# Gate and up products by blocks (seven products for eight) from the third chunk on, two of four sums of weight blocks by accumulating DMAs

## The chip, the cores and the metric

One core of one Trainium2 chip runs the whole program. The metric is device microseconds of one execution, from start to end; lower is better. The engines are TensorE (PE), VectorE (DVE), ScalarE (ACT), GpSimd (POOL) and SyncE (SP); each works through its own row of instructions in order, and they wait for each other by semaphores.

## The reference

Two decoder layers on 512 tokens of width 1024 in float32: a gated short convolution in the first, dilated window attention in the second, and behind each a gated feed-forward part, which is what the change touches:

```python
def swiglu(x, w_gate_up, w_down):
    g, u = jnp.split(x @ w_gate_up, 2, axis=-1)
    return (jax.nn.silu(g) * u) @ w_down
...
    f = swiglu(rms_norm(h, ffn_norm_pre[layer]), ffn_w_gate_up[layer], ffn_w_down[layer])
    h = h + rms_norm(f, ffn_norm_post[layer])
```

Here x is 512 x 1024, w_gate_up is 1024 x 5632 (gate and up, 2816 columns each) and w_down is 2816 x 1024.

## The kernel before

Every product keeps float32 accuracy by splitting both operands in two fp32r parts, a high one (a cast on ACT) and a low one (a subtraction on DVE): `split` (L91), and `parts` (L104) for weights. A product is then three matmuls: high by high, low by high, high by low. The input x lies in SBUF by features, as `xh` and `xl` in tiles of 128 features by 128 tokens.

`ffn` (L394) walks through 11 chunks of 256 gate columns and the 256 up columns that belong to them. `load_cols` (L124) fetches each 1024 x 256 piece by one DMA of 1 MB on SP into `raw`, of which there are two buffers (`wp`). `makers` (L197) splits it in halves of 128 columns, and `feature_mm` (L135, matmuls in L160) makes the products: for each half 8 pieces of features x 3 matmuls, 128 columns of weights standing, 512 tokens moving, gate and up in turn, each into a PSUM bank of its own (tags mm and at, four banks each). For one half of a chunk ACT makes the silu and DVE the product with up:

```python
                    s = apool.tile([P, T], F32, tag="silu", name="s", bufs=2)
                    nc.scalar.activation(s, ps[2 * j], AF.Silu)
                    nc.vector.tensor_tensor(act[2 * c + j], ps[2 * j + 1], s, ALU.mult)
```

The first chunk is made in token halves, between which the last two transposes of x (`Next.x`, L326) are put (`Next.rest`, L337). After the chunks `down` (L348) multiplies by w_down. Split weights lie in tiles with six buffers each of high and low.

A scheduler sets each engine's row when the program is built; matmuls issued through `strict` (L130) stay in the order of the code. A semaphore holds back an instruction and with it all that stands behind it on its engine.

Of the kernel before, what the change touches and what calls it, by code (L numbers as in the profile page):

```python
# [15 lines left out]
P = 128  # L16
# [22 lines left out]
def trunk(  # L39
# [27 lines left out]

    xp = [keep.tile([P, KT * T], F32R, name=n, align_bytes=LINE) for n in ("xh", "xl")]  # L70
# [5 lines left out]
    cst = keep.tile([P, 576], F32, name="cst")  # L76
# [11 lines left out]
    def bank(tag, name):  # L88
        return psum.tile([P, T], F32, tag=tag, name=name)
# [14 lines left out]
    def parts(src, gain=None, pool=wp, bufs=6):  # L104


        _, a, b = src.shape
        wh = pool.tile([P, a, b], F32R, tag="wh", name="wh", bufs=bufs, align_bytes=LINE)
        wl = pool.tile([P, a, b], F32R, tag="wl", name="wl", bufs=bufs, align_bytes=LINE)
        if gain is None:  # L110
            split(wh, wl, src)
            return wh, wl
        for i in range(a):
            g = gain[:, i:i + 1]
            nc.scalar.mul(wh[:, i], src[:, i], g)  # L115
            nc.vector.scalar_tensor_tensor(  # L116
                wl[:, i], src[:, i], g, wh[:, i].bitcast(F32), ALU.mult, ALU.subtract)
        return wh, wl
# [272 lines left out]
                    after.after_half(tt, n)  # L391
        return after

    def ffn(layer, pending, after):  # L394
        w = ffn_w_gate_up[layer]
        with ExitStack() as phase:
            apool = phase.enter_context(tc.tile_pool(name=f"a{layer}", bufs=4))
            act = []
            for n, bufs in ((1, NF - 12), (0, 12)):
# [3 lines left out]
                act = [pool.tile([P, T], F32, tag=f"act{k}", name="act")  # L403
                       for k in range(bufs)] + act
            for c in range(NF // 2):
                rg = load_cols(w, c * 256)
                ru = load_cols(w, DFF + c * 256)
                mg, mu = makers("mm", rg), makers("at", ru)
                rest = pending.rest() if c == 0 else {}
                if c == 1:  # L410
                    rest["marks"] = [pending.made[NT - 1]] * 4
                ps = feature_mms([mg[0], mu[0], mg[1], mu[1]], **rest)
                for j in range(2):
                    s = apool.tile([P, T], F32, tag="silu", name="s", bufs=2)
                    nc.scalar.activation(s, ps[2 * j], AF.Silu)  # L415
                    nc.vector.tensor_tensor(act[2 * c + j], ps[2 * j + 1], s, ALU.mult)  # L416
# [14 lines left out]
    with ExitStack() as phase:  # L431
# [57 lines left out]
        for c in range(KT // 2):  # L489
# [58 lines left out]
    pending = ffn(0, pending, lambda ys: Next(npool, ys, ffn_norm_post[0], None))  # L548

# [380 lines left out]
```

## Time and profile before

| | |
|---|---|
| median of 3 runs | 1476.7 us (1476.43 to 1477.5) |
| profiled execution | 1476.04 us, its span 1474.3 us |
| PE busy | 1459.1 us, 99% of the span |
| DVE / ACT / POOL busy | 692.6 / 657.8 / 57.3 us |
| DMA traffic | 137.44 MB, mean 93 GB/s |

The rows in the section further down come from several views. The page gives sums over the execution. The stage table gives for each stretch (start:end, length) the busy time and number of instructions of PE, PE's weight loads, DVE, ACT and POOL, then the mean granted clock of PE (1.00 is full), the share of the DMA engines and GB/s. The timeline gives start, duration, engine, line, operation, output<-inputs, shape and number of instructions merged in one row; in brackets the idle time before and what ended it. The groups by line give count, then busy us and mean ns of one. Durations of neighbours overlap: what an engine can do in a row shows in the distance of the starts.

### The profile page before, as it was taken

Reading aid. Unit: us, or ns where it says so; the run is one execution under the profiler, and the core shown is the slowest. Engines: PE = TensorE matmul, PEld = TensorE weight load, DVE = VectorE, ACT = ScalarE, POOL = GpSimd, SP = SyncE. Lnnn points to the kernel's source line nnn. Section 1 sums busy time; section 2 is a strip of 40 time slices with the busy share of each in tenths; the row PEclk is TensorE's granted clock in tenths of the full one; section 3 lists DMA queues with packets and bytes.
Section 4 is the critical chain, followed back from the end, with each engine's and each line's share of the span. In section 5 each row is a group of like instructions: output and inputs, shape, how many; then the busy total and the mean of one; then the engine's idle time right before and its main releaser. Section 6 shows DMA issues by size and latency. Waiting matters only on the chain.

```text
span 1474.3 us, 20308 instructions
## 1 busy us (share of the span) xinstructions
PE 1459.1 (99%) x8160; PEld 1247.3 (85%) x8160; DVE 692.6 (47%) x1381; ACT 657.8 (45%) x1337; POOL 57.3 (4%) x108
## 2 busy tenths in 40 slices
PE   9999999999999999999999999999999999999998
PEld 7888898888888889898899889889789888888886
DVE  5644453232223446767457555745545323223433
ACT  4313342222222336896677768768444222222321
POOL 1000100000000010010000001001010000000000
PEclk9999999999999999999999999999999999999999
DMA  6333123233232312322212312312113331332311
GB/s 217 114 116 114 57 91 107 89 114 103 83 127 102 116 56 70 125 66 92 94 46 87 111 62 60 115 58 60 58 58 115 114 110 62 114 128 94 107 57 57
DMA packets 110516, 137.44 MB, mean 93 GB/s; under 512 B 3502, under 2 KB 99286, under 8 KB 110423
## 3 DMA queue, kind: packets, MB, share of 16 engines
q1 hardware_dynamic: 108852, 135.69, 28.0%
q8 instruction: 64, 1.05, 0.3%
q0 software_dynamic: 1280, 0.26, 0.3%
q14 instruction: 30, 0.24, 0.1%
q10 hardware_dynamic: 290, 0.20, 0.0%
HBM read 133.92 MB, written 2.23 MB: 92 GB/s over the span
## 4 chain that ended last, share of the span: by engine, by line
PE 72%; issue 25%; DVE 1%; POOL 1%; ACT 1%; DMA 0%; SPq 0%; POOLq 0%; DVEq 0%; ACTq 0%
PE mmf L133 16%; PE atf L160 15%; PE mmf L160 12%; PE vps L133 10%; PE s L133 2%; PE tr L133 2%; PE o L133 2%; PE y L133 1%; PE tr L283 1%; PE y2b L231 0%; PE y3b L231 0%; PE y2b L227 0%; PE y3b L227 0%; PE y3b L229 0%; PE y2a L231 0%
## 5 line engine op out<-in xcount | busy, mean ns | idle before, releaser
L94 DVE TENSOR_TENSOR wl<-raw,wh 128x1024 fp32r<-128x1024 f32 x176 | 210.7, 1223 | 70.1 <-ACT wh L93 69.7
L93 ACT CAST wh<-raw 128x1024 fp32r<-128x1024 f32 x176 | 178.1, 1046 | 75.9 <-PE atf L160 43.1
L160 PE MATMUL atf<-xh,wh 128*128 128x512 f32 (+1 forms) x560 | 181.0, 366 | 0.0
L160 PE MATMUL atf<-xh,wl 128*128 128x512 f32 (+1 forms) x560 | 180.4, 365 | 0.0
L160 PE MATMUL atf<-xl,wh 128*128 128x512 f32 (+1 forms) x560 | 180.0, 365 | 0.0
L415 ACT ACTIVATE s<-mmf 128x512 f32<-128x512 f32 x44 | 26.3, 598 | 330.3 <-PE mmf L160 322.1
L416 DVE TENSOR_TENSOR act<-atf,s 128x512 f32<-128x512 f32 x44 | 30.4, 692 | 297.3 <-ACT s L415 297.3
L116 DVE SCALAR_TENSOR_TENSOR wl<-raw,cols,wh 128x256 fp32r<-128x256 f32 x272 | 115.8, 483 | 104.2 <-ACT wh L115 104.2
L160 PE MATMUL mmf<-xh,wh 128*128 128x512 f32 (+1 forms) x496 | 162.1, 365 | 0.6 <-ACT xh L93 0.6
L160 PE MATMUL mmf<-xl,wh 128*128 128x512 f32 (+1 forms) x496 | 160.4, 362 | 0.0
L160 PE MATMUL mmf<-xh,wl 128*128 128x512 f32 (+1 forms) x496 | 160.3, 362 | 0.0
L115 ACT ACTIVATE wh<-raw,cols 128x256 fp32r<-128x256 f32 x272 | 115.0, 498 | 65.5 <-PE mmf L133 46.9
L160 PEld LDWEIGHTS atf<-xh,wh 128*128 128x128 f32 x560 | 99.6, 189 | 16.7
L160 PEld LDWEIGHTS atf<-xh,wl 128*128 128x128 f32 x560 | 99.6, 189 | 16.8
L160 PEld LDWEIGHTS atf<-xl,wh 128*128 128x128 f32 x560 | 99.5, 189 | 16.9
L133 PE MATMUL mmf<-xh,wh 128*128 128x512 f32 x352 | 110.7, 396 | 0.0
L133 PE MATMUL mmf<-xh,wl 128*128 128x512 f32 x352 | 108.8, 390 | 0.0
L133 PE MATMUL mmf<-xl,wh 128*128 128x512 f32 x352 | 108.5, 390 | 0.0
L160 PEld LDWEIGHTS mmf<-xh,wh 128*128 128x128 f32 x496 | 88.6, 191 | 15.6 <-ACT xh L93 1.1
L160 PEld LDWEIGHTS mmf<-xl,wh 128*128 128x128 f32 x496 | 87.5, 189 | 14.4
L160 PEld LDWEIGHTS mmf<-xh,wl 128*128 128x128 f32 x496 | 87.5, 189 | 14.3
L93 ACT CAST ah<-act 128x512 fp32r<-128x512 f32 x44 | 27.1, 620 | 117.5 <-PE y3b L229 116.0
(202 smaller groups left out, 2455.8 us busy)
## 6 DMA issues: line engine op xcount, KB each, us to landing
raw<-in_ffn_w_gate_up SPq DMA_DIRECT2D x44, 1024.0 KB, 6.6
raw<-in_w_kv SPq DMA_DIRECT2D x24, 1024.0 KB, 5.2
raw<-in_ffn_w_down SPq DMA_DIRECT2D x22, 1024.0 KB, 4.8
raw<-in_w_q SPq DMA_DIRECT2D x12, 1024.0 KB, 5.1
raw<-in_conv_w_in SPq DMA_DIRECT2D x11, 1024.0 KB, 5.3
raw<-in_conv_w_out SPq DMA_DIRECT2D x4, 1024.0 KB, 4.9
raw<-in_w_o SPq DMA_DIRECT2D x4, 1024.0 KB, 5.1
h<-in_x SPq DMA_DIRECT2D x4, 512.0 KB, 7.3
```

The costliest lines, as they stand in the source:

```text
L93: return [nc.scalar.copy(hi, src).ins, nc.vector.tensor_tensor(lo, src, hi.bitcast(F32), ALU.subtract).ins]
L94: nc.vector.tensor_tensor(lo, src, hi.bitcast(F32), ALU.subtract).ins]
L115: nc.scalar.mul(wh[:, i], src[:, i], g)
L116: nc.vector.scalar_tensor_tensor(wl[:, i], src[:, i], g, wh[:, i].bitcast(F32), ALU.mult, ALU.subtract)
L133: traced[:] = [op(*args, **kwargs).ins]
L160: nc.tensor.matmul(*args, **kwargs)
L283: nc.tensor.transpose(ps[:, k, :], hn[:, c][:, k * P:(k + 1) * P], ident)
L415: nc.scalar.activation(s, ps[2 * j], AF.Silu)
L416: nc.vector.tensor_tensor(act[2 * c + j], ps[2 * j + 1], s, ALU.mult)
```

## The change

Chunks 0 and 1 stay. From chunk 2 on each side (gate or up of one chunk) is a `Pair`: the 1024 x 256 weights are taken as four blocks of 512 x 128 (W11, W12 in the upper half of the features, W21, W22 in the lower), x as four blocks of 512 features x 256 tokens, and seven products of sums of blocks take the place of eight products of blocks. `sums_of_x` makes the four sums of x once a layer. Of the weights' four sums two are adds on DVE (L407), and two are DMAs issued by POOL (L415) that read a block from DRAM a second time and add it onto a block in `raw`: W12 onto W22, and W11 onto W12. The results are put together from PSUM by copies on ACT and adds on DVE. Tiles that were two are one (x, w), two constants are trimmed, and the norm pool is closed before chunk 2 and opened again after the last.

```diff
...
-        wh = pool.tile([P, a, b], F32R, tag="wh", name="wh", bufs=bufs, align_bytes=LINE)
-        wl = pool.tile([P, a, b], F32R, tag="wl", name="wl", bufs=bufs, align_bytes=LINE)
+        w = pool.tile([P, 2 * a, b], F32R, tag="w", name="w", bufs=bufs, align_bytes=LINE)
+        wh, wl = w[:, 0:a], w[:, a:2 * a]
...
+            n1, n2 = raw[:, :, 0:P], raw[:, :, P:2 * P]
+            k1, k2 = slice(0, KT // 2), slice(KT // 2, KT)
+            def add(out, a, b):
+                nc.vector.tensor_tensor(out, a, b, ALU.add)
+            a1 = parts(n1)
+            a22 = [pool.tile([P, KT // 2, P], F32R, tag="ah", name=n, align_bytes=LINE)
+                   for n in ("dh", "dl")]
+            split(*a22, n2[:, k2])
+            for k, i, j in ((k2, 0, 1), (k1, 0, 0)):
+                nc.gpsimd.dma_start(n2[:, k], src[i * T:(i + 1) * T, j * P:(j + 1) * P].rearrange(
+                    "(k p) n -> p k n", p=P), accum_op=ALU.add)
+            add(n1[:, k1], n1[:, k1], n2[:, k2])
+            add(n1[:, k2], n1[:, k2], n1[:, k1])
+            s1 = parts(n1)
+            s2 = parts(n2)
+            self.w = {
+                1: [z[:, k1] for z in a1], 2: [z[:, k2] for z in a1],
+                6: [z[:, k1] for z in s1], 3: [z[:, k2] for z in s1],
+                7: [z[:, k1] for z in s2], 5: [z[:, k2] for z in s2], 4: a22}
+            self.z, self.x, self.y = (bank(t, n)[:, 0:T // 2] for t, n in (
+                ("mm", "z"), ("mm", "zx"), ("at", "zy")))
+            self.r = pool.tile([P, T], F32, tag="al", name="r", align_bytes=LINE)
+            self.r2 = pool.tile([P, T], F32, tag="al", name="r2", align_bytes=LINE)[:, 0:T // 2]
+        def product(self, out, n, first, last):
+            w, x = self.w[n], self.xs[n]
+            out = out.rearrange("p (t n) -> p t n", n=P)
+            for k in range(KT // 2):
+                for p in range(3):
+                    strict(nc.tensor.matmul, out, w[p == 1][:, k, :], x[p == 2][:, :, k, :],
+                           start=first and k + p == 0, stop=last and k == KT // 2 - 1 and p == 2,
+                           skip_group_check=True)
+        def p1(self):
+            self.product(self.z, 1, True, True)
+            nc.scalar.copy(self.r[:, 0:256], self.z)
+        def p2(self):
+            self.product(self.x, 2, True, True)
+            nc.vector.tensor_tensor(self.r[:, 0:256], self.x, self.r[:, 0:256], ALU.add)
+        def p6(self):
+            self.product(self.z, 6, False, True)
+            nc.scalar.copy(self.r[:, 256:512], self.z)
...
+        def p7(self):
+            self.product(self.z, 7, False, True)
+            nc.scalar.mul(self.r2, self.z, -1.0)
+        def c22(self):
+            nc.vector.tensor_tensor(self.r2, self.r2, self.y, ALU.subtract)
+            g = self.gate
+            if g is None:
+                self.s2 = self.pool.tile([P, T], F32, tag="silu", name="s2", bufs=2)
+                nc.scalar.activation(self.s2[:, 256:512], self.r2, AF.Silu)
+            else:
+                nc.vector.tensor_tensor(
+                    self.act[:, 768:1024], self.r2, g.s2[:, 256:512], ALU.mult)
...
+        def p3(self):
+            self.product(self.y, 3, False, True)
+            nc.vector.tensor_tensor(self.r[:, 256:512], self.y, self.r[:, 256:512], ALU.add)
...
+        b11, b12, b21, b22 = (t.rearrange("p (t k n) -> p t k n", t=2, n=P) for t in scratch)
+        for out, k, t in ((b11, 0, 0), (b12, 0, 1), (b22, 1, 1), (b21, 1, 0)):
+            nc.vector.tensor_tensor(
+                out, *(block(z, k, t).bitcast(F32) for z in (xh, xl)), ALU.add)
+        nc.vector.tensor_tensor(b11, b11, b12, ALU.subtract)
+        nc.vector.tensor_tensor(b12, b22, b12, ALU.subtract)
+        nc.vector.scalar_tensor_tensor(b22, b11, -1.0, b22, ALU.mult, ALU.subtract)
+        nc.vector.scalar_tensor_tensor(b21, b22, -1.0, b21, ALU.mult, ALU.subtract)
...
+            norms.close()
+            with tc.tile_pool(name=f"sums{layer}", bufs=1, side="right") as sums:
+                xs = sums_of_x(sums, act[-4:])
+                before = None
+                for c in range(2, NF // 2):
+                    gate = None
+                    for raw, c0 in zip(loads(c), starts(c)):
+                        p = Pair(apool, raw, w[:, c0:c0 + 256], xs, gate, act[c])
+                        p.p1()
+                        if gate and c == NF // 2 - 1:
+                            before.p4()
+                            p.p6()
+                            before.p3()
+                            p.p7()
+                            p.p2()
+                            p.p5()
+                            p.c22()
+                            p.p4()
+                            p.p3()
+                            break
+                        p.p2()
+                        if before:
+                            before.p4()
+                        p.p6()
+                        if before:
+                            before.p3()
+                        p.p5()
+                        p.p7()
+                        p.c22()
+                        before = gate = p
+            npool = norm_pool(norms, f"{layer}f")
...
```

How the rows of the engines changed, at three places. The names carry the program's numbers; rows of one side have the same raw.

DVE in a middle chunk of the first layer. Before, where raw_2212 and raw_2214 are the next chunk's gate and up, raw_2338 and raw_2340 those behind it, and act the products:

```order
L416 TENSOR_TENSOR act_1577<-atf_1979,s_2083 128x512 [waits PE_49,Activation_49]
L94 TENSOR_TENSOR wl_2218<-raw_2212,wh_2217 128x1024 [waits DMAHW6_49,Activation_49]
L94 TENSOR_TENSOR wl_2223<-raw_2214,wh_2222 128x1024 [waits DMAHW7_49,Activation_49]
L416 TENSOR_TENSOR act_1578<-atf_2095,s_2206 128x512 [waits PE_49,Activation_49]
L94 TENSOR_TENSOR wl_2228<-raw_2212,wh_2227 128x1024 [waits DVE_49,Activation_49]
L94 TENSOR_TENSOR wl_2233<-raw_2214,wh_2232 128x1024 [waits DVE_49,Activation_49]
L416 TENSOR_TENSOR act_1579<-atf_2105,s_2209 128x512 [waits PE_49,Activation_49]
L94 TENSOR_TENSOR wl_2344<-raw_2338,wh_2343 128x1024 [waits DMAHW0_49,DVE_49,Activation_49]
L94 TENSOR_TENSOR wl_2349<-raw_2340,wh_2348 128x1024 [waits DMAHW1_49,DVE_49,Activation_49]
```

Low parts are made a half chunk at a time, each pair behind a product, and nothing in the row depends on a pair just made. After, one turn, from p2 of one side (r_2278) to p2 of the next (r_2398): L95 are subtractions that make low parts, L407 the adds, raw_2140 is the side that PE works on, raw_2374 the next:

```order
L446 TENSOR_TENSOR r_2278<-zx_2276,r_2278 128x256 [waits PE_49,Activation_49]
L95 TENSOR_TENSOR w_2269<-raw_2140,w_2269 128x1024 [waits Activation_49]
L95 TENSOR_TENSOR w_2272<-raw_2140,w_2272 128x1024 [waits DMASW5_49,Activation_49]
L95 TENSOR_TENSOR w_2378<-raw_2374,w_2378 128x1024 [waits DMAHW6_49,Activation_49]
L95 TENSOR_TENSOR dl_2382<-raw_2374,dh_2381 128x512 [waits PE_49,Activation_49]
L480 TENSOR_TENSOR r_2162<-zy_2161,r_2162 128x256 [waits PE_49]
L460 TENSOR_TENSOR r2_2279<-r2_2279,zy_2277 128x256 [waits Activation_49]
L407 TENSOR_TENSOR raw_2374<-raw_2374 128x4x128 [waits DMASW1_49,DVE_49]
L466 TENSOR_TENSOR act_1537<-r2_2279,s2_2256 128x256 [waits DVE_49]
L407 TENSOR_TENSOR raw_2374<-raw_2374 128x4x128 [waits DVE_49]
L446 TENSOR_TENSOR r_2398<-zx_2396,r_2398 128x256 [waits PE_49,Activation_49]
```

Four subtractions and two products a chunk become, for each side, the low parts of its two sums (w_2269, w_2272), the low parts of the next side (w_2378, dl_2382) and its two adds, with the evacuations between; the first add waits for a DMA of POOL (DMASW).

POOL in the feed-forward part of the first layer. Before, the norm's small operations end and the next layer's norm follows:

```order
L251 TENSOR_TENSOR y_1534<-a_1532,mhalf_74 128x1 [waits DVE_49,Pool_49]
L249 TENSOR_SCALAR a_1544<-ssx_1538 128x1 [waits Activation_49]
L251 TENSOR_TENSOR y_1546<-a_1544,mhalf_74 128x1 [waits DVE_49,Pool_49]
L249 TENSOR_SCALAR a_3734<-ssn_3708 128x1 [waits Activation_49]
L251 TENSOR_TENSOR y_3736<-a_3734,mhalf_74 128x1 [waits DVE_49,Pool_49]
```

Nothing of POOL stands beside the gate and up products. After, between the same two, two transfers for each side; three sides of them:

```order
L415 DMA raw_2374<-in_ffn_w_gate_up 128x4x128 [waits DMAHW6_49,DMASW6_49,DMASW4_49]
L415 DMA raw_2374<-in_ffn_w_gate_up 128x4x128 [waits DVE_49]
L415 DMA raw_2376<-in_ffn_w_gate_up 128x4x128 [waits DMAHW7_49,DMASW7_49,DMASW5_49]
L415 DMA raw_2376<-in_ffn_w_gate_up 128x4x128 [waits DVE_49]
L415 DMA raw_2610<-in_ffn_w_gate_up 128x4x128 [waits DMAHW0_49,DMASW1_49,DMASW0_49]
L415 DMA raw_2610<-in_ffn_w_gate_up 128x4x128 [waits DVE_49]
```

The first of a side waits for the load alone (DMAHW; the DMASW are of the buffer's user before), the second for DVE, which is the subtraction into dl.

PE at the start of a chunk's second half before (mmf gate, atf up):

```order
L160 MATMUL mmf_2090<-xh_66,wh_2091 128x512 [waits PE_49,Activation_49]
L160 MATMUL atf_2095<-xh_66,wh_2096 128x512 [waits Activation_49]
L160 MATMUL mmf_2090<-xh_66,wl_2092 128x512 [waits DVE_49]
L160 MATMUL atf_2095<-xh_66,wl_2097 128x512 [waits DVE_49]
L160 MATMUL mmf_2090<-xl_67,wh_2091 128x512
L160 MATMUL atf_2095<-xl_67,wh_2096 128x512
```

All its weights are ready there, since both low parts were made a half chunk ahead. After, in the side of raw_2140 from the end of p4 of the side before, over p6 (z_2275 with w_2269), p3 of the side before, p5 and p7:

```order
L134 MATMUL z_2159<-x_66,dh_2145 128x256 x2
L134 MATMUL z_2159<-x_66,dl_2146 128x256
L134 MATMUL z_2159<-x_66,dh_2145 128x256
L134 MATMUL z_2275<-xs_1920,w_2269 128x256 [waits Activation_49]
L134 MATMUL z_2275<-xs_1920,w_2269 128x256 [waits DVE_49]
L134 MATMUL z_2275<-xs_1920,w_2269 128x256 x10
L134 MATMUL zy_2161<-x_66,w_2153 128x256 x12
L134 MATMUL zy_2277<-xs_1920,w_2272 128x256 [waits Activation_49]
L134 MATMUL zy_2277<-xs_1920,w_2272 128x256 [waits DVE_49]
L134 MATMUL zy_2277<-xs_1920,w_2272 128x256 x10
L134 MATMUL z_2275<-xs_1920,w_2272 128x256 [waits Activation_49]
L134 MATMUL z_2275<-xs_1920,w_2272 128x256 x11
```

Matmuls of 512 columns became runs of 12 matmuls of 256 columns; the first of p6 waits for ACT's cast and the second for DVE's subtraction of the same side's sum.

## Rows read from the trace of the kernel before

**Rows 1.** Page, parts 1 and 4: busy time of each engine; the chain by engine.
```profile
PE 1459.1 (99%) x8160; PEld 1247.3 (85%) x8160; DVE 692.6 (47%) x1381; ACT 657.8 (45%) x1337; POOL 57.3 (4%) x108
PE 72%; issue 25%; DVE 1%; POOL 1%; ACT 1%; DMA 0%; SPq 0%; POOLq 0%; DVEq 0%; ACTq 0%
```

**Rows 2.** Stage table: gate and up of both layers, and a stretch at attention's end.
```profile
213.00:398.00 185.00, 185.00 (x838) 154.08 (x838) 57.53 (x58) 47.06 (x58) 0.00 (x0) 1.00 0.33 105
1135.00:1310.00 175.00, 175.00 (x774) 144.96 (x773) 51.77 (x52) 41.89 (x51) 0.00 (x0) 1.00 0.31 100
...
1000.00:1050.00 50.00, 46.63 (x398) 44.45 (x397) 32.54 (x114) 38.20 (x104) 5.88 (x10) 0.97 0.23 70
```

**Rows 3.** Timeline of PE, gate and up, first and last of 91 starts.
```profile
250.64 0.39 PE L160 MATMUL mmf<-xh,wh 128*128 128x512 f32 x1
...
271.04 0.39 PE L160 MATMUL mmf<-xh,wh 128*128 128x512 f32 x1
```

**Rows 4.** Timeline of ACT in the same stage.
```profile
294.14 0.60 ACT L415 ACTIVATE s<-mmf 128x512 f32<-128x512 f32 x1 [8.40 <-PE mmf L160]
...
305.02 0.60 ACT L415 ACTIVATE s<-mmf 128x512 f32<-128x512 f32 x1 [8.40 <-PE mmf L160]
```

**Rows 5.** Timeline of PE where token halves are made (attention's first products).
```profile
558.17 1.12 PE L160 MATMUL mmf<-xh,wl 128*128 128x256 f32 x8
559.13 1.12 PE L160 MATMUL mmf<-xl,wh 128*128 128x256 f32 x8
```

**Rows 6.** Timeline of DVE, gate and up.
```profile
294.77 0.69 DVE L416 TENSOR_TENSOR act<-atf,s 128x512 f32<-128x512 f32 x1 [7.58 <-ACT s L415]
295.70 2.36 DVE L94 TENSOR_TENSOR wl<-raw,wh 128x1024 fp32r<-128x1024 f32 x2 [0.24 <-ACT wh L93]
```

**Rows 7.** Groups by line, shapes apart: DVE, ACT, PE.
```profile
L94 DVE TENSOR_TENSOR wl<-raw,wh 128x1024 fp32r<-128x1024 f32 x176 | 210.7, 1223 | 70.1 <-ACT wh L93 69.7
L94 DVE TENSOR_TENSOR al<-act,ah 128x512 fp32r<-128x512 f32 x44 | 30.2, 691 | 98.0 <-ACT ah L93 98.0
L669 DVE CUSTOM_DVE_ANT_0 p<-s,cst 128x256 f32<-128x256 f32 x112 | 41.4, 420 | 0.2 <-PE s L133 0.2
L741 ACT COPY v<-vps 32x256 f32<-32x256 f32 x64 | 23.2, 363 | 0.8
L160 PE MATMUL mmf<-xl,wh 128*128 128x256 f32 x128 | 21.1, 283 | 0.0
```

**Rows 8.** Tile d (attention's statistics): POOL's issue of the 16 KB transfers, ns.
```profile
L692 POOL DMA_DIRECT2D d<-st x4: 760/760/762, 659.3 to 1028.3; - x4
```

**Rows 9.** Page, part 6: DMA issues, count, KB each, median us to landing.
```profile
raw<-in_ffn_w_gate_up SPq DMA_DIRECT2D x44, 1024.0 KB, 6.6
...
out<-h SPq DMA_DIRECT2D x7, 256.0 KB, 2.1
...
d<-st POOLq DMA_DIRECT2D x4, 16.0 KB, 2.2
```

**Rows 10.** Line 101 (loads), 200 to 400 us.
```profile
DMA to landing us min/median/max: 5.1/7.6/8.2
```

**Rows 11.** Page, part 3: SP's queue: packets, MB, share of 16 engines.
```profile
q1 hardware_dynamic: 108852, 135.69, 28.0%
```

**Rows 12.** Timeline of DVE from the convolution's end to the first chunk.
```profile
193.68 0.69 DVE L315 TENSOR_TENSOR yg<-y3b,grow 128x512 f32<-128x512 f32 x1 [1.50 <-ACT junk L243]
...
198.12 1.42 DVE L272 SCALAR_TENSOR_TENSOR hn<-h,y,grow 128x512 f32<-128x512 f32 x2 [0.84 <-POOL y L251]
...
206.34 1.29 DVE L94 TENSOR_TENSOR xl<-tr,xh 128x512 fp32r<-128x512 f32 x2 [4.46 <-ACT xh L93]
```

**Rows 13.** Timeline of PE, the last transposes of x.
```profile
205.09 1.03 PE L283 MATMUL tr<-ident,hn 128*128 128x128 f32 x8
```

**Rows 14.** Timeline of PE behind its one long idle time.
```profile
1045.48 1.97 PE L133 MATMUL tr<-ident,p 128*128 128x128 f32 x8 [3.37 <-DVE p L755]
```

More of the change, by code (lines that the diff above doesn't have):

```diff
@@ L66, in trunk @@
     psum = ctx.enter_context(tc.tile_pool(name="psum", bufs=4, space=PSUM))
-    xp = [keep.tile([P, KT * T], F32R, name=n, align_bytes=LINE) for n in ("xh", "xl")]
+    xp = keep.tile([P, 2 * KT * T], F32R, name="x", align_bytes=LINE)
+    xp = [xp[:, n * KT * T:(n + 1) * KT * T] for n in range(2)]
     xh, xl = (t.rearrange("p (t k n) -> p t k n", t=NT, n=P) for t in xp)
@@ L392, in down, with __init__, p5, p4 @@
         return after
-    def ffn(layer, pending, after):
+    class Pair:
+        def __init__(self, pool, raw, src, xs, gate, act):
+            self.pool, self.xs, self.gate, self.act = pool, xs, gate, act
+            n1, n2 = raw[:, :, 0:P], raw[:, :, P:2 * P]
[38 more added lines that the diff above has]
+            nc.scalar.copy(self.r[:, 256:512], self.z)
+        def p5(self):
+            self.product(self.y, 5, True, True)
+        def p7(self):
[10 more added lines that the diff above has]
+                    self.act[:, 768:1024], self.r2, g.s2[:, 256:512], ALU.mult)
+        def p4(self):
+            self.product(self.z, 4, False, True)
+            g = self.gate
+            if g is None:
+                nc.scalar.activation(self.s2[:, 0:256], self.z, AF.Silu, scale=-1.0)
+            else:
+                nc.vector.scalar_tensor_tensor(
+                    self.act[:, 512:768], self.z, -1.0, g.s2[:, 0:256], ALU.mult, ALU.mult)
+        def p3(self):
+            self.product(self.y, 3, False, True)
+            nc.vector.tensor_tensor(self.r[:, 256:512], self.y, self.r[:, 256:512], ALU.add)
+            g = self.gate
+            if g is None:
+                self.s1 = self.pool.tile([P, T], F32, tag="silu", name="s1", bufs=2)
+                nc.scalar.activation(self.s1, self.r, AF.Silu)
+            else:
+                nc.vector.tensor_tensor(self.act[:, 0:512], self.r, g.s1, ALU.mult)
@@ new lines, in block, with sums_of_x @@
+    def block(z, k, t):
+        return z[:, 2 * t:2 * t + 2, 4 * k:4 * k + 4, :]
+    def sums_of_x(pool, scratch):
+        b11, b12, b21, b22 = (t.rearrange("p (t k n) -> p t k n", t=2, n=P) for t in scratch)
[6 more added lines that the diff above has]
+        nc.vector.scalar_tensor_tensor(b21, b22, -1.0, b21, ALU.mult, ALU.subtract)
+        homes = pool.tile([P, 6 * D], F32R, name="xs", align_bytes=LINE).rearrange(
+            "p (c e t k n) -> p c e t k n", c=3, e=2, t=2, n=P)
+        homes = [[homes[:, c, e] for e in range(2)] for c in range(3)]
+        xs = {n: [block(z, k, t) for z in (xh, xl)]
+              for n, k, t in ((1, 0, 0), (2, 1, 0), (3, 1, 1), (4, 0, 1))}
+        for n, src in ((6, b22), (5, b11), (7, b12), (4, b21)):
+            if n not in xs:
+                xs[n] = homes.pop()
+            split(*xs[n], src)
+        return xs
@@ L395, in ffn @@
+    def ffn(layer, pending, norms, after):
         w = ffn_w_gate_up[layer]
@@ L402, in ffn, with loads, starts @@
                 pool = stack.enter_context(actp)
-                act = [pool.tile([P, T], F32, tag=f"act{k}", name="act")
+                act = [pool.tile([P, 2 * T], F32, tag=f"act{k}", name="act")
                        for k in range(bufs)] + act
-            for c in range(NF // 2):
-                rg = load_cols(w, c * 256)
-                ru = load_cols(w, DFF + c * 256)
+            def loads(c):
+                return [load_cols(w, c0) for c0 in starts(c)]
+            def starts(c):
+                return [c0 + c * 256 for c0 in (0, DFF)]
+            for c in range(2):
+                rg, ru = loads(c)
                 mg, mu = makers("mm", rg), makers("at", ru)
@@ L421, in held_pool @@
                 return stack.enter_context(tc.tile_pool(name=f"held{layer}", bufs=2))
-            return down(apool, act, ffn_w_down[layer], held_pool, after)
+            halves = [a[:, j * T:(j + 1) * T] for a in act for j in range(2)]
+            return down(apool, halves, ffn_w_down[layer], held_pool, lambda ys: after(npool, ys))
     def norm_pool(stack, n):
```

16 lines of the change are left out of this document (9 added, 7 removed).

## The prediction

> **What bounds the kernel now.** I read the page from the top: busy times, the chain that ended last, the stage table, and then the timeline of single engines inside one chunk. TensorE (PE) is busy for 1459.1 of 1474.3 us and gives 72% of the chain, with 25% "issue" between its own matmuls; no other engine is over half busy [rows 1]. The stage that changes is the gate and up products, from about 213 to 398 us and again from 1135 to 1310 us: there PE has no gap, its granted clock is 1.00 (2.4 GHz), and DVE works 57.5 of 185 us, ACT 47.1 [rows 2]. So a chunk costs what its matmuls cost. The reader should take the pitch, not the duration, of a matmul: 90 matmuls of 512 columns start between 250.64 and 271.04 us, which is 226.7 ns each [rows 3]. ACT's silu comes every 10.88 us, twice a chunk [rows 4], and 48 x 226.7 ns is the same 10.88 us. I call the gate or the up part of a chunk a side; before, a side costs 10.88 us of PE and nothing else.
>
> **The change, part by part.** *Matmuls.* A side had 48 matmuls of 512 columns and now has seven products of 12 matmuls, 84 in all, of 256 columns. The same shape runs now in the transitions: eight start in 0.96 us, 120 ns each [rows 5]. So 84 x 120 = 10.08 us instead of 10.88, 0.80 us a side; 36 sides (9 chunks x 2 x 2 layers) would give 28.8 us if PE went on without gaps. The fixed 13 ns of each matmul is now paid 84 times, which is why an eighth less columns is only a fourteenth less time.
>
> *What a side asks of DVE and ACT.* Before: two casts and two subtractions of 128x1024, a silu or product. Now three such pairs, one of 128x512 (dh, dl), two adds of 128x512, and four to six pieces out of PSUM. On DVE three of 1.14 us pitch (two subtractions in 2.36 us, one lasting 1.22 [rows 6]), 0.69 for dl and for each add [rows 7], and about four pieces at 0.42 [rows 7]: some 7.2 of 10 us. Capacity is there; order decides.
>
> *The ring on DVE.* The order rows show it: DVE does, in this row, s1 and s2 of side n, a1 and dl of side n+1, then the two adds of side n+1, which give s1 of side n+1 its input. The first add waits for the accumulating transfer that adds W12 into W22 (I call it A), and A waits on POOL for dl. PE's p6 of side n+1 waits for s1. So each side must go once round: s1, s2, a1 at 1.14 = 3.42; dl 0.69; A from issue to landing, D; add 0.69, add 0.69; on every second side a product (0.42) between them, 0.21 on average; the cast of s1 on ACT 1.05 [rows 7]; six handovers at 0.03 (silu ends at 294.74, its product starts at 294.77 [rows 4, 6]), 0.18. That is 6.9 + D a side. Queued behind the waiting add on DVE are p2's evacuation and s1, and behind those, on PE, p6: a late A stops everything.
>
> *How long A takes, D.* No accumulating transfer stands in the trace. From below: POOL's own transfers with the same number of pieces (128 partitions x 4) take 0.76 us of POOL [rows 8] and land 2.2 us after issue with 16 KB [rows 9]; A moves 16 times the bytes, so D is not under 2.2. From above: a plain load of 1 MB, four times the bytes, lands in at most 8.2 us in this stage, median 7.6 [rows 10]. Between: SP's queue used 28.0% of 16 engines for 108,852 packets of 135.69 MB [rows 11], that is 6605 us of engine time, 60.7 ns a packet of 1.25 KB, some 25 ns for 512 B. A has 512 pieces of 512 B, 32 an engine, 0.8 us a pass; it has to read its source and its target, so two passes, 1.6 us. 2.2 + 1.6 = 3.8. Meanwhile the next 1 MB load runs: it is issued when s2 is done, some 1.9 us before A, and lands in 5.1 us at best [rows 10], so it shares the engines for about the first half of A's data; I add 0.7. **D = 4.5 us**, nearest to the 16 KB row plus data; both ends, 2.2 and 8.2, are kept for the range. The other transfer (W11 into W12, B) needs only the load, is issued earlier, and is waited for last by s2: hidden, as it has a whole side.
>
> By the Trainium skill, "DMA: Bandwidth & Descriptors", section "Anatomy of one DMA", a transfer issued from GpSimd takes about 2.0 us plus its bytes over 436 GB/s; for 256 KB that is an estimate of 2.6 us, and no run shows it yet for accumulation. With it the sum would be that of the first rival below, 1464.
>
> *The ring through PE.* A second chain bounds from below, whatever D is: after s1's subtraction, PE has 47 more matmuls to the end of p7 (5.64 us) and 0.16 us until the last ends (duration 0.28 [rows 7] less the pitch); ACT's copy of p7 0.36 and DVE's c22 0.42 [rows 7], then both adds stand behind c22 on DVE (1.38, and 0.21), cast 1.05, subtraction 1.22; with eight handovers 10.7, less 0.1 as the add needs only DVE's pitch behind c22: 10.6 us a side. So a side costs the larger of 10.6 and 6.9 + D, not 10.08.
>
> *Start and end.* The sums of x (eight DVE instructions and four splits a layer, 13.7 us of DVE) lie beside chunks 0 and 1, where PE has 10.9 + 21.8 us of its own work. Two of them stand ahead of the last rows' norm: DVE idles there 1.50, 0.84 and 4.46 us, and the last normed row is done at 199.5 while PE transposes it at 205.1 [rows 12, 13]. So 2.3 us of adds cost nothing; without that cover 4.6 us for both layers. The first two sides of each layer are made ready during chunk 1 and run at PE's own 10.08. Merged tiles, smaller constants and the norm pool opened again move no long instruction: nothing.
>
> **Sum.** 6.9 + 4.5 = 11.4 us a side, 0.52 over the old 10.88. 32 sides x 0.52 = +16.6; 4 sides x 0.80 = -3.2; together +13.4 us. The profiled execution took 1476.0 us (span 1474.3 and 1.7 around it), 0.7 below the median of the runs, 1476.7; so 1489.4 against the one and **1490 us** against the other, slower by 0.9%. It breaks even at D = 4.1.
>
> **The rivals.**
> 1. *A lands in time* (other sign). If A takes 3.7 us or less, the ring through PE decides: 32 x -0.28 - 3.2 = -12 us, **1464**. For it: the 16 KB transfer's 2.2 us, and 256 KB stored by SP in 2.1 us [rows 9]. Against: two reads and a load beside it. It turns at D = 4.1. Chance 0.31.
> 2. *A is as slow as a load.* With D = 6.6, the median of all gate and up loads [rows 9], a side takes 13.5 us: 32 x 2.62 - 3.2 = +81, **1557**. For it: adding in flight could cost more than a second read, and loads in this stage land in up to 8.2 us. Against: a quarter of the bytes. Chance 0.22.
> 3. *PE alone bounds* (the waits I read into the order fall into gaps): 36 x -0.80 = **1448**. Against: the order itself, in which DVE cannot reach s1 before c22 and the adds. Chance 0.03.
> 4. *The change gives back what it saves*, D near 4.1: 1474 to 1480. Chance 0.07.
>
> The stalls, about a microsecond a side, hardly touch the clock: after the one idle of 3.37 us in the trace [rows 14] the mean clock of its 50 us is still 0.97 [rows 2].
>
> **How the numbers follow.** The forecast, D from 4.2 to 5.6, has 0.37. I count 0.2% (3 us) as what a measurement of this kernel can tell. Faster: 0.31 + 0.03 = 0.34; same 0.07; slower 0.37 + 0.22 = 0.59. Both signs hold much of the chance; the forecast's own range is 1480 to 1525 (D = 5.6: 32 x 1.62 - 3.2 = +49). The range of 8 in 10 takes in rival 1 with a little for shorter handovers, 1462, and rival 2 up to D = 6.85, 1565; what lies outside is PE alone (0.03) and D over 6.85 (about 0.13).
>
> **What would show it.** Matmuls of 256 columns at a pitch of 120 ns within a product, with a gap on PE at the second matmul of p6 in each side; DVE's first add idle before it with the transfer into raw as releaser; the landing time of that transfer near 4.5 us; sides at 11.4 us. If c22 is what the add waits for and the sides lie at 10.6, rival 1 holds; if the gap lies elsewhere, for instance at p1 for a late raw load, my ring is the wrong one.

## The result and the profile after

1527.3 us, median of 4 runs (1525.0 to 1532.1), against 1476.6 before: ratio 1.035, 95% interval 1.032 to 1.037, 50.8 us slower. The profiled execution took 1525.0 us. The prediction had the sign and the place, but not the size: +13.4 us. The measured time lies inside the wide range (8 chances in 10) of 1462 to 1565 us, and 2 us above the forecast's own 1480 to 1525.

The page of the changed kernel, parts 1, 3, 4 and 6, answers to [rows 1, 9, 11]:

```profile
span 1523.2 us, 23581 instructions
PE 1457.5 (96%) x9456; PEld 1300.6 (85%) x9456; DVE 869.6 (57%) x1675; ACT 765.2 (50%) x1543; POOL 152.5 (10%) x180
q1 hardware_dynamic: 108852, 135.69, 26.9%
q0 software_dynamic: 39296, 19.14, 10.5%
PE 69%; DMA 11%; DVE 11%; issue 5%; ACT 3%; POOL 1%; DVEq 0%; POOLq 0%; SPq 0%; ACTq 0%
raw<-in_ffn_w_gate_up SPq DMA_DIRECT2D x44, 1024.0 KB, 5.2
raw<-in_ffn_w_gate_up POOLq DMA_DIRECT2D x72, 256.0 KB, 4.7
```

PE is busy about as long as before (1457.5 against 1459.1 us), though it has less to multiply: the same matmuls take 1432.6 us in a run below in which nothing holds them up, so some 25 us of its busy time here come with the gaps. The chain that ended last has 11% of DMA and 11% of DVE in it, which had 0% and 1%. The stage table answers to [rows 2]: its lines are the two stages of sides and two stretches of one of them (PE, PEld, DVE, ACT, POOL busy with counts, granted clock, DMA share, GB/s).

```profile
240.00:458.00 218.00, 192.98 (x1501) 187.19 (x1500) 128.58 (x185) 95.77 (x155) 41.04 (x32) 0.97 0.59 131
1177.00:1394.00 217.00, 192.09 (x1491) 186.20 (x1490) 128.87 (x185) 94.82 (x154) 41.09 (x32) 0.97 0.60 131
300.00:350.00 50.00, 44.74 (x337) 43.54 (x337) 29.85 (x43) 22.16 (x36) 10.29 (x8) 0.93 0.63 131
350.00:400.00 50.00, 44.41 (x353) 42.61 (x352) 31.24 (x45) 23.03 (x39) 10.26 (x8) 1.00 0.61 127
```

PE idles 25 us in each stage, where it had no gap. One side on DVE (timeline: start, us; in brackets the idle time before and what ended it), between two runs of dl:

```profile
316.07 0.69 DVE L95 TENSOR_TENSOR dl<-raw,dh 128x512 fp32r<-128x512 f32 x1
...
321.85 1.42 DVE L407 TENSOR_TENSOR raw<-raw 128x512 f32<-128x512 f32 x2 [1.41 <-DMA raw<-in_ffn_w_gate_up]
...
324.37 3.50 DVE L95 TENSOR_TENSOR w<-raw,w 128x1024 fp32r<-128x1024 f32 x3 [0.78 <-ACT w L94]
327.79 0.68 DVE L95 TENSOR_TENSOR dl<-raw,dh 128x512 fp32r<-128x512 f32 x1
...
334.42 0.69 DVE L407 TENSOR_TENSOR raw<-raw 128x512 f32<-128x512 f32 x1 [1.99 <-DMA raw<-in_ffn_w_gate_up]
```

This is the forecast ring, row by row: dl, the wait for A, two adds, the cast of s1 on ACT, then s1, s2 and the next a1 in 3.42 us (324.37 to 327.79). But from dl's end to the first add it is 5.09 us in the one side (316.76 to 321.85) and 5.95 in the next (328.47 to 334.42). Over both layers A ends that wait in 24 of 30 sides: 4.84 to 6.90 us, mean 5.38 (the other six end with ACT's copy of p7 or DVE's own row); forecast were 4.5 and two handovers, 4.56. From dl to dl a side takes 12.27 us (mean of 29). A itself lands 4.9 us after its issue (mean of 31 sides, 4.45 to 6.58). POOL's two issues of A in the same sides, and the landing time of all 72 accumulating transfers:

```profile
317.20 1.30 POOL L415 DMA_DIRECT2D raw<-in_ffn_w_gate_up  x1 [7.60 <-DVE r L480]
328.77 1.28 POOL L415 DMA_DIRECT2D raw<-in_ffn_w_gate_up  x1 [6.48 <-DVE dl L95]
DMA to landing us min/median/max: 4.4/4.7/6.7
```

POOL starts 0.44 and 0.30 us after dl's end, not 0.03 (mean 0.35), and an issue takes it 1.28 us; [rows 8] have 0.76. PE waits where it was foretold, at the first matmul of p6 for the cast and at the second for the subtraction:

```profile
325.66 1.58 PE L134 MATMUL z<-xs,w 128*128 128x256 f32 x11 [0.87 <-DVE w L95]
...
337.18 0.39 PE L134 MATMUL z<-xs,w 128*128 128x256 f32 x1 [1.31 <-ACT w L94]
338.44 2.52 PE L134 MATMUL z<-xs,w 128*128 128x256 f32 x11 [0.87 <-DVE w L95]
```

The last row is a surprise: eleven matmuls in 2.52 us instead of 1.58. The granted clock is at its lower level there, 1.2 GHz, until about 342 us (stage table by microseconds):

```profile
339.00:340.00 1.00, 1.00 (x7) 1.00 (x6) 1.00 (x2) 0.54 (x2) 0.00 (x0) 0.50 0.00 0
```

Between 250 and 440 us that happens three times, each time behind a gap in front of p6.

### The profile page after: what moved, and what is told of

It reads as the page before. It is cut to its first block, busy times and chain, and to the rows that moved or that the text cites. A ratio compares the mean times of both kernels' runs of the same rounds, so it can differ in the third digit from the quotient of the medians.

```text
span 1523.2 us, 23581 instructions
## 1 busy us (share of the span) xinstructions
PE 1457.5 (96%) x9456; PEld 1300.6 (85%) x9456; DVE 869.6 (57%) x1675; ACT 765.2 (50%) x1543; POOL 152.5 (10%) x180
## 3 DMA queue, kind: packets, MB, share of 16 engines
q0 software_dynamic: 39296, 19.14, 10.5%
## 4 chain that ended last, share of the span: by engine, by line
PE 69%; DMA 11%; DVE 11%; issue 5%; ACT 3%; POOL 1%; DVEq 0%; POOLq 0%; SPq 0%; ACTq 0%
PE mmf L134 16%; DMA raw<-in_ffn_w_gate_up 10%; PE vps L134 8%; PE atf L161 8%; PE mmf L161 5%; DVE w L95 5%; PE z L134 3%; DVE raw L407 3%; ACT w L94 2%; PE zy L134 2%; PE s L134 2%; PE tr L134 2%; PE o L134 2%; DVE dl L95 1%; PE y L134 1%
## 5 line engine op out<-in xcount | busy, mean ns | idle before, releaser
L95 DVE TENSOR_TENSOR w<-raw,w 128x1024 fp32r<-128x1024 f32 x212 | 252.9, 1220 | 76.3 <-ACT w L94 75.4
L94 ACT CAST w<-raw 128x1024 fp32r<-128x1024 f32 x212 | 213.0, 1045 | 157.6 <-DVE raw L407 69.6
L134 PE MATMUL mmf<-x,w 128*128 128x512 f32 x1056 | 246.5, 391 | 0.0
L134 PEld LDWEIGHTS mmf<-x,w 128*128 128x128 f32 x1056 | 196.2, 188 | 39.4
L134 PE MATMUL z<-xs,w 128*128 128x256 f32 x864 | 133.0, 301 | 49.9 <-DVE w L95 23.5
L161 PE MATMUL atf<-x,w 128*128 128x512 f32 (+1 forms) x816 | 174.7, 340 | 0.0
L161 PEld LDWEIGHTS atf<-x,w 128*128 128x128 f32 x816 | 134.8, 190 | 16.8
L134 PE MATMUL vps<-w,x 128*128 128x256 f32 x1152 | 142.3, 284 | 0.0
L134 PEld LDWEIGHTS vps<-w,x 128*128 128x128 f32 x1152 | 139.1, 192 | 1.9
L161 PE MATMUL mmf<-x,w 128*128 128x256 f32 (+1 forms) x624 | 131.7, 327 | 1.0 <-ACT x L94 0.6
L415 POOL DMA_DIRECT2D raw<-in_ffn_w_gate_up x72 | 92.8, 1325 | 387.1 <-DVE dl L95 200.0
L161 PEld LDWEIGHTS mmf<-x,w 128*128 128x128 f32 x624 | 99.7, 192 | 11.5 <-ACT x L94 1.3
L95 DVE TENSOR_TENSOR al<-act,ah 128x512 fp32r<-128x512 f32 x44 | 30.2, 690 | 90.2 <-ACT ah L94 90.0
L407 DVE TENSOR_TENSOR raw<-raw 128x512 f32<-128x512 f32 x72 | 49.6, 690 | 55.5 <-DMA raw<-in_ffn_w_gate_up 54.8
L763 ACT COPY sw<-mmf 32x512 f32<-32x512 f32 x92 | 53.2, 578 | 30.1 <-PE mmf L134 18.8
```

The lines of the kernel that those rows point to most:

```text
L94: return [nc.scalar.copy(hi, src).ins, nc.vector.tensor_tensor(lo, src, hi.bitcast(F32), ALU.subtract).ins]
L95: nc.vector.tensor_tensor(lo, src, hi.bitcast(F32), ALU.subtract).ins]
L134: traced[:] = [op(*args, **kwargs).ins]
L161: nc.tensor.matmul(*args, **kwargs)
L407: nc.vector.tensor_tensor(out, a, b, ALU.add)
L415: nc.gpsimd.dma_start(n2[:, k], src[i * T:(i + 1) * T, j * P:(j + 1) * P].rearrange("(k p) n -> p k n", p=P), accum_op=ALU.add)
```

## The experiments

Theory: the ring of the prediction holds, 6.9 us and the wait for A; A takes longer than the 4.5 us it was given. Rivals: the ring through PE with its clock falls; DVE's load; the traffic of the transfers as such. The scheduler makes the rows anew for every version, and in the versions with sums moved to DVE its row has another order too. So these show that a kernel without A on the ring is fast; what A's time is worth with the row left as it is, two others show: plain copies (the same rows on DVE and ACT) and the small POOL instruction (the same in the steady sides).

**All four sums on DVE; B alone there; no transfers at all.** Three runs that take transfers away. In place of the loop of `dma_start` that issues both:

```diff
...
+            add(n2[:, k2], n2[:, k2], n2[:, k1])
+            add(n2[:, k1], n2[:, k1], n1[:, k1])
...
```

the second line alone, with A kept; and neither line nor transfer.

> Both accumulating transfers become additions on DVE (0.69 us each), of tiles that are in SBUF already. Theory (the ring on DVE through transfer A sets the side): the ring loses D and POOL's handovers, 5.4 us in the trace of the changed kernel, and gains two additions, 1.4 us; what is left is DVE's own work, 3.4 + 5 x 0.69 + some four pieces of 0.42 + 1.1 us for the cast of s1, about 10 us, and PE's 10.08, so a side costs 10.1 to 10.6 us and the run 1449 to 1467 us; no idle of DVE behind a transfer. Rival (the ring through PE, c22 and the additions decides, or DVE's load does): DVE has more to do and nothing is won, 1520 us or more. Rival (traffic of the transfers delays the raw loads): also fast, but the run without A's rival below tells it apart.

> Only transfer B (W11 into W12) becomes an addition on DVE; A stays. Theory (A's landing is on the ring, B's is not): dl to the first addition stays near 5 us, a little under the 5.4 of the changed kernel, since half of the accumulating traffic is gone; the addition of 0.69 us falls into DVE's wait for A; 1505 to 1527 us. Rival (the traffic or POOL's 1.28 us an issue decides): half of both is gone, so half of the loss, some 1500 us or less. Rival (DVE's load): slower than 1527, by up to 32 x 0.69 = 22 us.

> Both accumulating transfers are left out, and with them the two sums that they make (the products are then of other matrices; the count and the size of every other instruction stay). Theory: no transfer on the ring, DVE has 1.4 us less a side than with all four additions there; PE's 10.08 or the ring through PE at up to 10.6, so 1449 to 1467 us. If DVE's own load were near its limit, this run would be clearly faster than the one with four additions on DVE. Rival (ring through PE at 12 us by clock falls): 1520 or more.

Measured: 1454.8 us (ratio to before 0.985, 0.984 to 0.987), 1523.7 (1.032, 1.031 to 1.034) and 1448.5 (0.981, 0.979 to 0.982). With four additions on DVE, more work than in the changed kernel, 72.5 us vanish; with B gone and A kept, 3.7, hardly more than the runs of one kernel differ. So it is A, and neither DVE's load nor the traffic. Without transfers PE has no gap in these stages, and the time is that of the third rival of the prediction, 1448: the price of the arithmetic was right, only not to be had with A on the ring.

**A and B copy instead of accumulating** (`accum_op` left out).

> Both transfers keep place, size, queue and waits, but copy instead of accumulating (the sums are left out with that). Theory as forecast (the target has to be read too, one pass of 0.8 us more): D falls from 4.7 to about 3.9 us, the ring goes to about 11.4, 1500 us. If accumulation has no price of its own: 4.7 us and 1527 again, and D is the price of any 256 KB transfer with 512 pieces from POOL beside a load. If accumulation is the larger part: about 2.2 to 3 us, the ring through PE at 10.6 decides, 1465 to 1480.

1506.9 us (1.020, 1.019 to 1.022), 20.4 less. The queue of POOL's transfers, and the landing of A:

```profile
q0 software_dynamic: 7040, 19.14, 4.4%
DMA to landing us min/median/max: 3.3/4.0/5.8
```

The wait from dl to the first add is 4.77 us (27 sides), 0.61 less, and 32 x 0.61 = 19.5. So accumulation costs 0.6 us, near the 0.8 that the forecast gave its second pass; it is not what makes D long. The same bytes go in 5760 packets instead of 38,016 (the other 1280 were there before), 80 a transfer instead of 528, and POOL's issue takes 0.75 us instead of 1.28. With plain copies the kernel would still have lost 30 us.

**A quarter of the load beside A.** From the fourth chunk on (a further change in the code, not shown, keeps the transfers on POOL in the order of the changed kernel):

```diff
...
-                return [load_cols(w, c0) for c0 in starts(c)]
+                if c > 2:
+                    for raw, c0 in zip(fixed, starts(c)):
+                        src = w[:, c0:c0 + 256].rearrange("(k p) n -> p k n", p=P)
+                        nc.sync.dma_start(raw[:, 0:KT:4], src[:, 0:KT:4])
+                else:
+                    fixed[:] = [load_cols(w, c0) for c0 in starts(c)]
+                return fixed
...
```

> From the fourth chunk on only two of eight blocks of rows of the raw weights are loaded (256 KB instead of 1 MB, into the same two tiles; the rest stays what the side before left there, so the products are of other matrices). Both accumulating transfers, their order on POOL and every other instruction stay. Theory (in the trace of the changed kernel the load issued on SP 2 us before A holds all 16 DMA engines until 2 us after A's issue, and A's packets move only then; so D is the load's rest plus A's own data): with a quarter of the load A's packets move at once, D falls from some 5 us to 3.2 to 3.6, the ring on DVE to under 11, and the ring through PE at 10.6 takes over: 1470 to 1485 us. Rival (accumulation has its 4.7 us by itself): 1520 to 1527, D unchanged.

1509.9 us (1.022, 1.021 to 1.024): a miss. In the changed kernel the load's packets fill the engines until A's begin, and I had taken the one for the cause of the other. Here A is issued at 324.89 (the row holds two issues: A, and right behind it the next side's B), the load's last packets go before 326, and yet A's do not start at once (stage table by microseconds; the last two columns are the DMA share and GB/s):

```profile
324.89 2.62 POOL L417 DMA_DIRECT2D raw<-in_ffn_w_gate_up  x2 [8.96 <-DVE dl L95]
```

```profile
324.00:325.00 1.00, 1.00 (x11) 1.00 (x10) 0.77 (x2) 0.00 (x0) 0.11 (x1) 1.00 0.73 225
325.00:326.00 1.00, 1.00 (x11) 1.00 (x10) 0.25 (x1) 0.63 (x1) 1.00 (x1) 1.00 0.13 41
326.00:327.00 1.00, 1.00 (x10) 1.00 (x10) 0.00 (x0) 0.00 (x0) 0.95 (x2) 1.00 0.07 6
327.00:328.00 1.00, 1.00 (x11) 1.00 (x10) 0.00 (x0) 0.30 (x1) 0.51 (x1) 1.00 0.99 121
```

The engines stand all but empty for a microsecond and a half until some 2 us after the issue. The wait falls to 4.97 us (30 sides): what goes on beside A costs 0.4, the rest is A's own. The clock stays at 1.00 from 250 to 440 us, and the side is 11.88 us (in every second one DVE's first add stands ahead of c22 here, not behind it). The 0.4 is a mean of unlike sides. In 11 of the changed kernel's 31 sides a transfer of the instruction queue (q8, 16 KB) is under way beside A, and A lands after 5.37 us; in the other 20, after 4.65. With the short load it is 4.65 (10 sides) and 4.52 (20). So the load by itself costs about 0.1, and most of the 0.4 stands in sides with load and instruction transfer together. No run tested that.

**A off the ring.** In place of both transfers and the first addition, W22 is added into W12, which waits for the load alone, and what B made comes from a subtraction:

```diff
...
+            nc.gpsimd.dma_start(n2[:, k1], src[T:2 * T, P:2 * P].rearrange(
+                "(k p) n -> p k n", p=P), accum_op=ALU.add)
+            add(n1[:, k1], n1[:, k1], n2[:, k1])
+            nc.vector.tensor_tensor(n2[:, k2], n1[:, k1], n2[:, k2], ALU.subtract)
             add(n1[:, k2], n1[:, k2], n1[:, k1])
...
-                7: [z[:, k1] for z in s2], 5: [z[:, k2] for z in s2], 4: a22}
+                7: [z[:, k2] for z in s2], 5: [z[:, k1] for z in s2], 4: a22}
...
```

> One accumulating transfer of the same size stays, but off the ring: W22 is added into W12 (waits for the raw load alone, not for dl), and the sum W11 + W12, which B made, is now a subtraction on DVE (0.69 us). Theory (what cost time was the wait for dl in front of the transfer, not the transfer): DVE finds the sum ready, three additions of 0.69 a side, 1448 to 1460 us, about as with all four on DVE. Rival (accumulating transfers or POOL's issue of 1.28 us cost time by themselves, half of them are left): about 1500.

1448.8 us (0.981, 0.980 to 0.983): the fastest version with all its sums, 27.9 us under the kernel before, with an accumulating transfer of the same size in each side. Its stages on PE have no gap and the clock is 1.00:

```profile
240.00:424.00 184.00, 184.00 (x1519) 183.28 (x1518) 141.63 (x202) 98.62 (x157) 19.63 (x16) 1.00 0.52 131
1142.00:1324.00 182.00, 182.00 (x1501) 181.19 (x1500) 139.29 (x200) 95.68 (x153) 19.26 (x15) 1.00 0.53 137
```

It also shows a transfer with no load beside it, from its issue on POOL on, by microseconds as above:

```profile
322.38 1.28 POOL L413 DMA_DIRECT2D raw<-in_ffn_w_gate_up  x1 [7.81 <-DMA raw<-in_ffn_w_gate_up]
```

```profile
322.00:323.00 1.00, 1.00 (x11) 1.00 (x10) 0.56 (x2) 0.62 (x1) 0.61 (x1) 1.00 0.00 0
323.00:324.00 1.00, 1.00 (x11) 1.00 (x10) 1.00 (x2) 0.12 (x1) 0.67 (x1) 1.00 0.00 0
324.00:325.00 1.00, 1.00 (x10) 1.00 (x9) 0.97 (x3) 0.26 (x1) 0.00 (x0) 1.00 0.50 61
325.00:326.00 1.00, 1.00 (x11) 1.00 (x10) 0.97 (x3) 0.64 (x1) 0.00 (x0) 1.00 1.39 174
326.00:327.00 1.00, 1.00 (x11) 1.00 (x10) 1.00 (x2) 1.00 (x2) 0.00 (x0) 1.00 0.23 27
```

Nothing moves until 324.4, 2.0 us after the issue began; the data takes 2.2 us more, to about 326.6, and the transfer has landed at 326.84, 0.3 later; transfers of this run land 4.5 us after issue (median).

**A on DVE, B still accumulating.** The one line with `add(n2[:, k2], n2[:, k2], n2[:, k1])` in place of A's transfer.

> Only A becomes an addition on DVE; B (W11 into W12) stays an accumulating transfer, but must now wait for that addition, which reads W12. So a transfer behind dl stays on a ring, a shorter one: s2, a1 at 1.14, dl and the addition 0.69 each, 0.35 to POOL, D about 5, the cast of s2 1.05: some 10.1 us. Theory: so much as PE's own 10.08; 1452 to 1475 us. Rival (any accumulating transfer between DVE's work costs what A did): 1505 or more.

1493.8 us (1.011, 1.010 to 1.013): the direction held, not the size. B, behind that addition, is now on a ring of its own: issued at 321.98, landed at 326.40, so that ACT casts s2 at 326.47, and so on to the next issue at 333.11, 11.13 us:

```profile
321.98 1.27 POOL L414 DMA_DIRECT2D raw<-in_ffn_w_gate_up  x1 [10.16 <-DVE raw L407]
333.11 1.28 POOL L414 DMA_DIRECT2D raw<-in_ffn_w_gate_up  x1 [9.86 <-DVE raw L407]
```

```profile
326.47 1.99 ACT L94 CAST w<-raw 128x1024 fp32r<-128x1024 f32 x2 [2.12 <-DMA raw<-in_ffn_w_gate_up]
```

My 10.1 had left out the pieces that DVE evacuates between a1 and dl, two to four at 0.33.

**PE's share and the clock.** Two runs put more matmuls, of p2 once more, into the gap in front of p6 (`self.product(self.y, 2, True, True)`, and nine of its twelve).

> Twelve more matmuls of 256 columns ahead of p6 in each side: p2's product once more, into the bank that p5 starts afresh later; the output stays what it was. They run in the gap in which PE waits for s1. Theory (DVE's ring through A sets the side; the falls of the clock behind the gaps only use up slack): 36 x 12 x 0.12 = 52 us more of PE's work cost nothing, 1520 to 1530 us. If the falls of the clock (three seen in layer 0, 1.2 to 1.7 us each) are part of the loss, they vanish, as PE has less idle time, and it gets up to 10 us faster: 1515 to 1520. Rival (PE's own matmuls bound): 1527 + 52 = 1579.

> Nine more matmuls of 256 columns (1.08 us) ahead of p6 in each side instead of twelve, which leaves the order on ACT and DVE as in the changed kernel but for some rows of the first sides; with twelve, ACT's copy of p7 had come to stand behind the cast of s1, so that PE waited for A twice. Theory (DVE's ring through A sets the side; PE has slack in front of p6): 36 x 9 x 0.12 = 39 us more of PE's work cost little, 1520 to 1535. If the falls of the clock behind the gaps are a part of the loss: they get fewer, 1512 to 1520. Rival (PE's own work bounds as well): 1550 to 1566.

1546.8 us (1.047, 1.045 to 1.050) and 1536.1 (1.041, 1.039 to 1.042). The first is a miss: the longer program was given another order, ACT's copy of p7 stands behind the casts of the next side, and p4 waits for it, so that the gap lies in front of the fill:

```profile
317.44 0.39 PE L134 MATMUL z<-x,dh 128*128 128x256 f32 x1 [2.24 <-ACT r L457]
```

The second, too, has more of this than I had read from the order: ACT's copy of p1 comes behind the casts, and p6 of each layer's last side waits 3.75 and 4.17 us for it. But 39 us more of PE's work cost 8.7, the side is 12.37 us from dl to dl against 12.27, and between 250 and 440 us the clock falls once (behind 402 us) instead of three times. So PE has slack, and as far as this run tells, the falls that are gone gave nothing back.

**The slope of the ring.** dl made a second time, and a small POOL instruction between dl and A:

```diff
             split(*a22, n2[:, k2])
+            nc.vector.tensor_tensor(a22[1], n2[:, k2], a22[0].bitcast(F32), ALU.subtract)
```

```diff
+            late = nc.gpsimd.tensor_scalar(
+                r2[:, T - 1:T], a22[1][:, 0, 0:1].bitcast(F32), EPS, mhalf, ALU.add, ALU.add).ins
...
+                with tc.issue_after(late) if i < j else nullcontext():
```

> The subtraction that gives dl is done twice (0.69 us more on DVE a side, the same output), so transfer A is issued 0.69 us later. Theory (dl, A, the additions and s1 are one ring): 32 x 0.69 = 22 us longer, 1545 to 1555; where the order on DVE puts another piece between the two, up to 0.4 us more. Rival (there is slack: another chain, of PE or of the loads, sets the side): within 10 us of the changed kernel.

> One small POOL instruction that reads dl (128x1; such ones take 0.43 to 0.60 us in the changed kernel) is put between dl and transfer A; the order on PE and DVE stays row by row as in the changed kernel. In the run with dl done twice the second subtraction had come to stand behind p3's evacuation, which waits for PE, so that run did not tell the slope. Theory (A is on a ring of DVE, and D and its handovers count fully): 0.5 to 0.6 us a side, 32 x 0.55 = 18 us, 1540 to 1550; more if the longer gap lets the granted clock fall behind every side, as it did there, and PE comes onto the ring (each fall costs 1.2 to 1.7 us): up to 1575. Rival (slack, another chain decides): 1522 to 1532.

1590.4 us (1.077, 1.075 to 1.079), far over the 22 us of the theory, and 1544.5 (1.045, 1.044 to 1.047), 17.2 more. In the first, the second subtraction stands behind p3's evacuation (L480), which waits for PE; A waits for both:

```profile
325.45 0.42 DVE L480 TENSOR_TENSOR r<-zy,r 128x256 f32<-128x256 f32 x1 [1.41 <-PE zy L134]
325.80 0.68 DVE L413 TENSOR_TENSOR dl<-raw,dh 128x512 fp32r<-128x512 f32 x1
```

```profile
335.56 2.71 PE L134 MATMUL z<-xs,w 128*128 128x256 f32 x11 [0.87 <-DVE w L95]
338.07 2.76 PE L134 MATMUL zy<-x,w 128*128 128x256 f32 x12
```

There p6 and p3 are on A's ring and run at the lower clock behind almost every gap. So the falls, free in the changed kernel, should cost time here; no run of this order without them was made. The second keeps DVE's order. Its instruction takes 0.28 us (median of 36); from dl to the first add it is 5.59 us instead of 5.38, a side 12.51 instead of 12.27. So the wait counts one to one in the steady sides, 32 x 0.24 = 8 us. The rest of its 17 came where the layers begin: from the first matmul by blocks to the third side's dl it is 18.8 us instead of 13.9 in the first layer and 21.3 instead of 14.8 in the second. There the rows of DVE, ACT and POOL have another order too; I did not take it apart.

## Why the prediction was wrong in size

- **PE alone, 84 x 120 ns: right.** The pitch inside the products is 120 ns, and the runs in which nothing is waited for lie at 1448.5 and 1448.8, where the third rival said 1448. It had been held against that rival that DVE cannot reach s1 before c22 and the adds; with another order of DVE's row PE finds its weights ready.
- **The ring, 6.9 us and D: right.** Two of the six handovers in the 6.9 lie inside the wait for A, so 6.84 were forecast for the rest. The side less the wait from dl to the first add is 12.27 - 5.38 = 6.89 us; with plain copies 11.76 - 4.77 = 6.99, with the short load 11.88 - 4.97 = 6.91.
- **"D = 4.5 us" and the handovers at 0.03: the step that failed.** From dl to the first add it is 5.38 us, 0.8 over the forecast 4.56, and each microsecond counts 32 times. Half of the 0.8 is D, 4.9 us on average; the other half is POOL's start behind dl, 0.35 where I had put 0.03, and the like at the landing. By the pieces of D: for the start I had taken the 2.2 of the 16 KB transfer, and it is 2.0 until the first packet. "0.8 a pass", from 25 ns for 512 B, gave 1.6 us of data, and it is 2.2: q0's 10.5% of 16 engines, less the 0.3% of before, is 2486 us for 38,016 packets, 65 ns each. About 0.3 us pass from the last packet to landing. So A alone takes the 4.5 that I had reckoned with a load beside it, and what goes on beside it adds 0.4, where I had put 0.7. That D came so near to 4.5 is in part luck: the data was put too low and the sharing too high.
- **The sum.** 32 sides at 12.27 instead of 11.4 are 27.8 us of the 37.4 that the forecast fell short (50.8 less 13.4).
- **"Start and end": wrong too.** The first two sides of a layer don't run at 10.08: p6 of side 0 idles 1.37 us in the first layer and 2.30 in the second, p6 of the first layer's last side 2.41 us, that one with the lower clock behind it. Of the other 9.6 us the ends make up some 6.5: from the first matmul by blocks to the last a layer takes 224.6 and 224.4 us in the profiled execution, against 186.2 in each layer with A off the ring, 76.6 us more, and 32 x (12.27 - 10.08) = 70.1 of them are the steady sides. Another 2.3 is that the median lies so much over the profiled execution. Without transfers on the ring the gaps at the ends are gone. On PE's timeline of the changed kernel:

```profile
244.27 1.67 PE L134 MATMUL z<-xs,w 128*128 128x256 f32 x12 [1.37 <-issue]
...
446.73 0.38 PE L134 MATMUL z<-xs,w 128*128 128x256 f32 x1 [2.41 <-ACT w L94]
447.99 2.71 PE L134 MATMUL z<-xs,w 128*128 128x256 f32 x11 [0.88 <-DVE w L95]
```

- **The ring through PE, 10.6 us a side: not tested.** With A on the ring the other one is longer, and in the runs that free PE the rows have another order and the sides run at 10.08.
- **"The stalls hardly touch the clock": wrong as to the clock, right as to the time**, as far as the run with nine more matmuls tells; in the run with dl done twice, with A behind PE's p3, probably wrong in both.
- **The rivals.** What the first asked for, a D of 3.7 or less, can't be had from this transfer, which takes 4.5 alone, and neither can the 4.1 at which the sign turns. So the sign was no luck. The second, D = 6.6, had the reason half right: what goes on beside A does cost, 0.4 us.

By the Trainium skill, "DMA: Bandwidth & Descriptors", section "Anatomy of one DMA", the estimate for 256 KB was 2.6 us. The trace disagrees: 4.5 us alone with accumulation, and 4.0 us as a plain copy beside a load (3.3 at least). That section puts most of the fixed 2 us behind the data, in the receipt of the write; here 2.0 us lie ahead of the first packet and some 0.3 behind the last.

## What to carry to other kernels

Before a sum is moved from an engine to a transfer, ask what that transfer waits for: one that needed only a load cost nothing at 4.5 us, and one of the same size behind an engine's result set the pace, as its time and the rest of its ring came to more than PE's own work for a side. Where a transfer of an unseen kind stands on a ring, an error in its price is multiplied by the number of turns: 0.9 us a side became 28. And an algebra that asks less of PE (10.08 for 10.88 us a side) is worth its price only if the weights are ready: choose which of the sums are made from which, so that no transfer stands behind a split.

## What the runs showed of the hardware

- An accumulating transfer of 256 KB moves in 528 packets, 65 ns each on average, a copy by the same pieces in 80; POOL's issue takes 1.28 us instead of 0.75. The gain of leaving the addition out is still only 0.6 us.
- Of an accumulating transfer's 4.5 us, 2.0 pass before its first packet; in the changed kernel, with the engines full of a load, it is 2.0 to 2.2.
- In 11 of the changed kernel's 31 sides, with a transfer of the instruction queue (q8, 16 KB) under way, A lands after 5.4 us on average, in the other 20 after 4.7. No run tested that.
- Behind a gap in front of p6 the granted clock sometimes falls to half for the next dozen or two of matmuls, and the length of the gap alone does not tell when: it fell behind a gap of 0.98 and 0.88 us at 422.10 us, and stayed at 1.00 behind 1.16 and 0.88 at 409.64 and behind 1.45 and 0.87 at 1225.84:

```profile
422.10 0.38 PE L134 MATMUL z<-xs,w 128*128 128x256 f32 x1 [0.98 <-ACT w L94]
423.36 2.17 PE L134 MATMUL z<-xs,w 128*128 128x256 f32 x11 [0.88 <-DVE w L95]
...
1225.84 0.39 PE L134 MATMUL z<-xs,w 128*128 128x256 f32 x1 [1.45 <-ACT w L94]
1227.10 1.57 PE L134 MATMUL z<-xs,w 128*128 128x256 f32 x11 [0.87 <-DVE w L95]
```
